# Placing the read-back of softmax sums, the loads of their reciprocals, and h's block sums in a hybrid decoder block

## The chip, the cores and the metric

The kernel runs on one core of a Trainium2 chip. The metric is the device time of one execution in microseconds; lower is better. The profile of one execution gives the times of single instructions, in microseconds from the start of its span.

## The reference

One decoder block on a sequence of L = 16 + 1024 tokens (16 learned tokens ahead of 1024 real ones), width D = 1024, all in float32:

```python
h = rmsnorm(x, norm_g)
u_pool, z_pool, q, k, v, z_attn, f_logit, g_pool, g_attn = split(h @ w_in)
y_pool = causal_multiscale_pool(u_pool, pool_w, pool_scale) * silu(z_pool)     # windows 2, 4, 8, 16
log_f  = log_sigmoid(f_logit + b_forget)
y_attn = forgetting_attention(q, k, v, log_f) * silu(z_attn)                    # 8 heads of 64, causal softmax
merged = sigmoid(g_pool) * (y_pool @ w_up_pool) + sigmoid(g_attn) * (y_attn @ w_up_attn)
out    = rmsnorm(x + merged @ w_out, final_norm_g)[16:]
```

In the attention, logits are q.k/8 plus a running sum of log forget gates, and each row is divided by the sum of its exponentials. That division is what the first part of the change is about: the kernel forms the undivided outputs first and multiplies them by the reciprocals of the sums much later.

## The kernel before

**Precision.** Every float32 product is made of three matmuls: each operand is split into a rounded part (ScalarE copies it) and the rest (VectorE or GpSimd subtracts), and rounded×rounded, rounded×rest and rest×rounded are added up in PSUM.

**Start (lines 460 to 578).** Eight tiles of 128 tokens (and one of 16) are loaded (`norm_load`), normalised, transposed by TensorE and split into `hh` and `hl`. For each tile `norm_stat` lets ScalarE sum the squares and GpSimd form the root (`rstd`), then `norm_scale` (VectorE, two operations at L258) scales it, and `norm_t` transposes it (TensorE at L279), rounds it (ScalarE, `hh` at L281) and subtracts (VectorE, `hl` at L282). Between these stand the first head pair's projections: `todo` lists (q, k, v) for four stretches of tokens, twelve steps numbered n = 0 to 11. In this stretch each engine works its instructions in program order. Steps 4 to 11 also call `h_block`: VectorE adds or negates a block of `hh` and `hl` into a tile `f` (L174 or L176, 1024 columns wide) and SyncE stores it to DRAM (L177), for products formed later in a seven-product (Strassen-like) way. Step 4 besides issues the loads `wf`, `bfb`, `psc` and the next q weights (`early["q"]`), step 6 the next k weights, step 8 forms `wfs` from `wf`; each of steps 4 to 11 issues one DRAM to DRAM copy (`copies(1)`).

**Attention (lines 580 to 881).** Sixteen units (four head pairs, two heads, two halves of the queries). TensorE's idle time in a unit is filled with projections. The sums of exponentials of each unit go as `acc` to DRAM (`accd`).

**The seven rounds (lines 896 to 1251).** The remaining gates z and g are projected by seven rounds n of products over 512×512 blocks. `order` lists products (n, i), i = 0 to 5; 38 of the 42 stand in the loop below, the last four come after it. Each product is 12 matmuls of 128×512 (L1069). All engines work in program order here, SyncE's queue of transfers too:

```python
for x, e in enumerate(order[:38]):
    if x == 0:
        g_prod(order[0])
        g_prod(order[1])
    if 4 <= x + AH < 42:
        split_next(order[x + AH])     # AH = 4: weights of the product four further on
    if x + 2 < 38:
        g_prod(order[x + 2])          # TensorE: the product two further on
    for f in before.get(e, ()):
        f()
    run_due(x)
    if x:
        evict(order[x - 1])           # clears the bank of the product before
    if x % 3 == 2:
        g_flush()
    for f in extra.get(e, ()):        # what hangs on this chunk
        f()
```

`split_next` (w_split) rounds a product's weights on ScalarE (L1024) and subtracts on GpSimd (L1031) or, for every third product, on VectorE (L1028); when half a load is used up it issues the next load of weights (`graw`, L1012). `g_prod` writes to one of eight PSUM banks: products with i < 4 of rounds 0, 2, 5 and 6 have a bank of their own (`ga_`), all others go round four banks (`gb_`), so that product (3,2) uses the bank of (2,4), and (4,5) that of (4,1). `evict` clears a bank on ScalarE (L1074) for rounds 0, 3 and part of 2, and on VectorE (L1080) for (2,4), (2,5) and rounds 1, 4 and 5; round 4's are followed by a sum on GpSimd (L136). `h_in(n)` loads round n's blocks of h (L1017) and `h_split(n)` splits them (L1040, L1045).

The tables `before` and `extra` hang other work on the chunks. For the softmax sums these are:

```python
def sums_in():
    for p in range(4):
        nc.sync.dma_start(lall[32 * p:32 * p + 32], sums[4 * p:4 * p + 4]....)     # L990
def sums_out():
    nc.vector.tensor_reduce(rall..., lall..., axis=AX.X, op=ALU.add)                # L994
    nc.vector.reciprocal(rall, rall)                                                # L996
    nc.vector.transpose(fin[:, 320:], rall)                                         # L997
    nc.sync.dma_start(recs.rearrange("(b p) r -> p b r", p=128), rect)              # L998
def rc_in(p):
    RC[p] = rc = gp.tile([128, SEQ], F32, name="rc", tag="g")
    for e in range(2):
        rw = recs...[4 * e + p:4 * e + p + 1]
        nc.sync.dma_start(rc[rows(e)[0]], rw.to_broadcast([64, SEQ]))               # L929
def attn_norm(p):
    nc.vector.tensor_tensor(Y[p], Y[p], RC[p], op=ALU.mult)                         # L932
```

Ahead of them, `acc_in(k)` and `acc_sum(k)` for k = 0 to 7, from (0,1) to (2,0), read `accd` back, sum over the keys, and with k = 7 store `sums` to DRAM (L986); `sums_in` follows in (2,0). `attn_in(p)` loads the undivided outputs `Y[p]` (L917, L920), and `attn_out(p)`, which needs `attn_norm(p)`, comes after the rounds. `pool_chain(g)` (one step for each call of `steps_of`) and `pool_split(g)` form the pooling branch's operands on VectorE and ScalarE (L951, L958, L965, L966). Tiles `u`, `s2`, `y`, `rc`, `plh` and `pll` share a ring of 13 slots, tag "g".

**End (lines 1253 to 1480).** The up-projections with their gates, and the last product with the final norm.

Of the kernel before, what the change touches and what calls it, by code (L numbers as in the profile page):

```python
# [44 lines left out]
def r32(ap):  # L45
    return ap.bitcast(F32)
# [7 lines left out]
def tile_hybrid_block(ctx, tc, x, meta, norm_g, w_in, b_forget, pool_w, pool_scale,  # L54
# [98 lines left out]
    def hblock(d, blk):  # L153
        r, c = int(blk[0]) - 1, int(blk[1]) - 1
        return r32(d[c][:, :, 512 * r:512 * r + 512])

    def rows_of(t):
        return t.rearrange("(k p) c -> p k c", p=128)
# [11 lines left out]
    def h_block(blk, k):  # L170
        f = ap_.tile([128, 2, 512], F32, name="f", tag="s", bufs=6)
        hi, lo = [hblock(d, blk)[:, k:k + 2] for d in (hh4, hl4)]
        if blk in ("12", "21"):
            nc.vector.scalar_tensor_tensor(f, hi, -1.0, lo, op0=ALU.mult, op1=ALU.subtract)  # L174
        else:
            nc.vector.tensor_tensor(f, hi, lo, op=ALU.add)  # L176
        nc.sync.dma_start(rows_of(HS[{"12": "C", "21": "X"}.get(blk, blk)])[:, k:k + 2], f)  # L177
# [59 lines left out]
    def run(g):  # L237
        for _ in g:
            pass
# [4 lines left out]
    def norm_load(i):  # L244
        c0 = i * 128
        n = min(128, L - c0)
        xt = ap_.tile([128, D], F32, name="xt", tag="s", bufs=6)
        nc.sync.dma_start(xt[:n], meta if n < 128 else x2[c0:c0 + n, :])
        return xt
# [40 lines left out]
    def zero_q(p):  # L290
        for e in range(2):
            nc.gpsimd.memset(r32(QL[p, e])[rows(e)[1]], 0.0)
# [18 lines left out]
    def q_piece(p, w, c0, c1):  # L311
        ps = yield from g_proj(w, c0, c1)

        def hi(e, r):
            nc.scalar.activation(QA[p, e][r, c0:c1], ps[rows(e)[0]], AF.Copy, scale=0.125)

        def lo(e):
            a, _ = rows(e)
            nc.vector.scalar_tensor_tensor(QL[p, e][a, c0:c1], ps[a], 0.125, r32(QA[p, e][a, c0:c1]),
                                           op0=ALU.mult, op1=ALU.subtract)  # L320

        for e in range(2):
            hi(e, rows(e)[0])
            hi(e, rows(e)[1])
        for e in range(2):
            lo(e)

    def k_piece(p, w, t0, t1):
        ps = yield from g_proj(w, t0, t1)
        for e in range(2):  # L330
            a, o = rows(e)
            for c, d in keys_of(t0, t1):
                nc.scalar.activation(KA[p, e][a, d], ps[a, c], AF.Copy)
        for e in range(2):
            a, o = rows(e)
            for c, d in keys_of(t0, t1):
                nc.vector.tensor_tensor(KA[p, e][o, d], ps[a, c], r32(KA[p, e][a, d]), op=ALU.subtract)  # L337

    def v_piece(p, w, t0, t1):
        ps = yield from g_proj(w, t0, t1)  # L340
        for c, d in keys_of(t0, t1):
            nc.scalar.activation(VT[p][:, d], ps[:, c], AF.Copy)

    def v_alloc(p):
        for e in range(2):
            V[p, e] = ap_.tile([KB, NB, 2, 64], F32R, name="V", bufs=3)
# [138 lines left out]
    def split_hi(raw, pool, tag):  # L485
        hi = pool.tile([128, KO, 128], F32R, name="whi", tag=tag)
        nc.scalar.activation(hi, raw, AF.Copy)
        return hi
# [13 lines left out]
    def ntok(i):  # L502
        return min(128, L - 128 * i)
# [22 lines left out]
    for n, (kind, t0, t1) in enumerate(todo):  # L526
        if n + 4 < 8:
            xts[n + 4] = norm_load(n + 4)
        if kind == "q":
            run(q_piece(0, wq, t0, t1))  # L530
        elif kind == "k":
            run(k_piece(0, wk, t0, t1))
        else:
            g = v_piece(0, wv, t0, t1)
            run(g)
        i = {0: 2, 1: 3, 3: 4, 4: 5, 5: 8, 6: 6, 7: 7}.get(n)
        if i is not None:
            norm_t(i, xts[i], ntok(i))
        if n == 0:
            hv_ = split_hi(rv, gp, "g")  # L540
            wv = split_lo(rv, hv_, gp, "g")
            VT[0] = gp.tile([128, L], F32, name="vt", tag="g")
            v_alloc(0)
        i = {1: 4, 2: 5, 3: 8, 4: 6, 5: 7}.get(n)
        if i is not None:
            norm_scale(xts[i], ntok(i), norm_stat(xts[i], ntok(i)))
        if n == 2:
            zero_q(0)
        if n == 4:
            wf = at_.tile([128, KO, H], F32, name="wf", bufs=1)  # L550
            nc.sync.dma_start(wf, w_in2[:, :, COL_F:COL_F + H])
            nc.sync.dma_start(bfb, bass.AP(tensor=b_forget.tensor, offset=b_forget.offset, ap=[[0, 128], [1, H]]))
            nc.sync.dma_start(psc, pool_scale[0].rearrange("(g c) -> c g", c=128))
        if n == 8:
            wfs = at_.tile([128, KO, 2 * H], F32R, name="wfs", bufs=1)
            nc.vector.tensor_copy(wfs[:, :, :H], wf)
            nc.vector.tensor_tensor(wfs[:, :, H:], wf, r32(wfs[:, :, :H]), op=ALU.subtract)
        if n == 4:
            early["q"] = load_raw(COL_Q + 128)
        if n == 6:  # L560
            early["k"] = load_raw(COL_K + 128)
        if n > 3:
            h_block(("11", "12", "22", "21")[n // 2 - 2], n % 2 * 2)
            copies(1)
        if n == 7:
            pw = ap_.tile([128, 4, 128], F32, name="pw", tag="s", bufs=6)
            nc.sync.dma_start(pw, pool_w[0].rearrange("g c d -> c g d"))
        if n == 10:
            nc.scalar.activation(pwh, pw, AF.Copy)
            nc.gpsimd.tensor_tensor(pwl, pw, r32(pwh), op=ALU.subtract)  # L570
        if n in (4, 7, 10):
            run(v_blocks(0, *range(max(1, 2 * (n // 3) - 2), 2 * (n // 3))))
# [341 lines left out]
    def attn_in(p):  # L914
        y = gp.tile([128, SEQ], F32, name="y", tag="g")
        if p == 3:
            nc.sync.dma_start(y, spill["y", p])  # L917
        else:
            for e in range(2):
                nc.sync.dma_start(y[rows(e)[0]], spill["y", p][:64, SEQ * e:SEQ * e + SEQ])  # L920
        Y[p] = y
# [3 lines left out]
# [3 lines that stand above are left out]
            rw = recs.rearrange("(h c) r -> h (c r)", h=H)[4 * e + p:4 * e + p + 1]  # L928
# [4 lines that stand above are left out]
# [29 lines left out]
    def pool_split(g):  # L962
        u = chains[g][0]
        plh, pll = [gp.tile([128, SEQ], F32R, name=n, tag="g") for n in ("plh", "pll")]
        nc.scalar.activation(plh, u[:, NM:], AF.Copy)  # L965
        nc.vector.tensor_tensor(pll, u[:, NM:], r32(plh), op=ALU.subtract)  # L966
        chains[g] += [plh, pll]
# [46 lines left out]
    def h_in(n):  # L1014
        raw_h[n] = [wp.tile([128, 2, 512], F32, name="hraw", tag=t) for t in ("wh", "wl")]
        for k in range(2):
            nc.sync.dma_start(raw_h[n][k], rows_of(HSRC[n])[:, 2 * k:2 * k + 2])  # L1017
# [18 lines left out]
    def h_split(n):  # L1036
        op_h[n] = [[hq.tile([128, 2, 512], F32R, name="gh", tag="h") for _ in range(2)] for _ in range(2)]
        hi, lo = op_h[n]
        for k in range(2):
            nc.scalar.activation(hi[k], raw_h[n][k], AF.Copy, scale=-1.0 if n == 2 else 1.0)  # L1040
        for k in range(2):
            if n == 2:
                nc.vector.scalar_tensor_tensor(lo[k], raw_h[n][k], -1.0, r32(hi[k]), op0=ALU.mult, op1=ALU.subtract)
            else:
                nc.vector.tensor_tensor(lo[k], raw_h[n][k], r32(hi[k]), op=ALU.subtract)  # L1045
# [144 lines left out]
    def steps_of(g):  # L1190
        return lambda: next(g, None)

    c2_, c1_ = pool_chain(2), pool_chain(1)
# [15 lines left out]
        (2, 1): [steps_of(c2_), lambda: attn_in(2)],  # L1209
        (2, 2): [steps_of(c2_), steps_of(c1_)],  # L1210
        (2, 3): [steps_of(c1_), lambda: h_in(5)],
        (2, 4): [steps_of(c1_), sums_out, lambda: attn_in(3)],
        (2, 5): [lambda: rc_in(0), lambda: rc_in(1)],
        (3, 0): [steps_of(c0_)],
        (3, 1): [lambda: h_split(4)],
        (3, 2): [steps_of(c0_)],
        (3, 3): [lambda: pool_split(3)],
        (3, 4): [lambda: attn_norm(0), lambda: h_in(6)],
        (3, 5): [lambda: pool_split(2)],
        (4, 0): [lambda: attn_norm(1)],  # L1220
        (4, 1): [lambda: h_split(5)],
        (4, 2): [lambda: rc_in(2)],
        (4, 3): [lambda: pool_split(1)],
        (4, 4): [lambda: rc_in(3)],
        (5, 3): [lambda: h_split(6)],
# [283 lines left out]
```

## Time and profile before

| | |
|---|---|
| median of 3 runs | 729.25 us (725.02, 729.25, 729.87) |
| profiled execution, own time | 727.64 us |
| its span | 725.9 us |
| mean granted TensorE clock | 0.994 |
| TensorE busy | 708.0 us (98%) |
| VectorE, ScalarE, GpSimd busy | 518.1, 421.0, 343.4 us |
| seven rounds' products | about 410 to 556 us |

The span runs from the first instruction of the program to the last; the own time holds 1.7 us besides. In the timelines a row gives start, duration, engine, line, operation, what is written and read, shapes and count, and in brackets how long the engine was idle before and what ended that. PE is TensorE, PEld its weight loads, DVE is VectorE, ACT is ScalarE, POOL is GpSimd, SPq is SyncE's queue of transfers. A row can merge several instructions; its duration is then that of all.

### The profile page before, as it was taken

The page shows a single profiled execution, that of the slowest core. Times are in us where ns is not written, and L with a number is a line of the kernel's source. Part 1 is how long each engine was busy: PE and PEld are TensorE (multiplying, and loading weights), DVE is VectorE, ACT ScalarE, POOL GpSimd, SP SyncE. Part 2 cuts the span into 40 slices and gives each one's busy share as a digit, 9 for nine tenths or more (in the row PEclk, how much of TensorE's full clock was granted, in tenths as well). Part 3 has the DMA queues.
Part 4 walks back from the last instruction along what each step waited for, and adds up shares of the span by engine and source line. Part 5 has one row for each costly group of instructions (what it writes and reads, how often), then busy time and mean ns, then how long its engine had stood idle before and what let it go on. Part 6 is the DMA issues. An engine that isn't in the chain of part 4 may idle for free.

```text
span 725.9 us, 10889 instructions
## 1 busy us (share of the span) xinstructions
PE 708.0 (98%) x3613; PEld 610.9 (84%) x3613; DVE 518.1 (71%) x917; ACT 421.0 (58%) x928; POOL 343.4 (47%) x463
## 2 busy tenths in 40 slices
PE   8989999999999999999999999969999999999996
PEld 6987999998899888998888888848888888888885
DVE  5774488576888868786876927957857645888775
ACT  7654477676767768676667522445545423525445
POOL 5423247476275847466395922346982010006152
PEclk9999999999999999999999999989999999999999
DMA  9299977956534475546648369689607367771006
GB/s 310 45 273 357 330 258 175 214 121 161 127 100 101 134 207 118 145 102 158 167 133 223 84 228 315 181 223 329 183 30 258 113 223 247 247 246 59 0 1 232
DMA packets 95354, 129.89 MB, mean 179 GB/s; under 512 B 11457, under 2 KB 62657, under 8 KB 93266
## 3 DMA queue, kind: packets, MB, share of 16 engines
q1 hardware_dynamic: 91776, 110.32, 48.1%
q0 software_dynamic: 2224, 16.25, 12.0%
q10 hardware_dynamic: 1298, 2.63, 1.0%
q8 instruction: 28, 0.46, 0.3%
q14 instruction: 28, 0.23, 0.1%
HBM read 102.25 MB, written 58.39 MB: 221 GB/s over the span
## 4 chain that ended last, share of the span: by engine, by line
PE 85%; DMA 5%; DVE 5%; ACT 2%; issue 2%; POOL 0%; SPq 0%; POOLq 0%; ACTq 0%; DVEq 0%
PE pj L217 53%; PE pj L1389 8%; PE pj L1069 7%; PE po L793 5%; PE pt L1389 2%; PE pt L1069 2%; PE ps L729 2%; PE ps L728 2%; DMA sums<-ge 1%; DMA zp<-accd 1%; DMA graw<-gs 1%; PE pj L589 1%; PE pt L279 1%; DVE pl L775 1%; PE pj L729 1%
## 5 line engine op out<-in xcount | busy, mean ns | idle before, releaser
L217 PE MATMUL pj<-hh,whi 128*128 128x512 f32 (+3 forms) x576 | 127.2, 347 | 0.3 <-DVE ka L337 0.2
L217 PE MATMUL pj<-hh,wlo 128*128 128x512 f32 (+3 forms) x576 | 127.2, 346 | 0.0
L217 PE MATMUL pj<-hl,whi 128*128 128x512 f32 (+3 forms) x576 | 126.8, 345 | 0.0
L217 PEld LDWEIGHTS pj<-hh,whi 128*128 128x128 f32 x576 | 97.3, 188 | 10.8 <-PE pj L217 0.5
L217 PEld LDWEIGHTS pj<-hh,wlo 128*128 128x128 f32 x576 | 96.8, 188 | 10.0
L217 PEld LDWEIGHTS pj<-hl,whi 128*128 128x128 f32 x576 | 96.5, 188 | 9.7
L208 POOL TENSOR_TENSOR wlo<-raw,whi 128x256 fp32r<-128x256 f32 x100 | 74.4, 775 | 63.9 <-PE pj L217 22.3
L783 POOL TENSOR_TENSOR acc<-acc,S 128x256 f32<-128x256 f32 (+2 forms) x128 | 90.6, 727 | 8.3 <-ACT S L770 4.1
L775 DVE TENSOR_TENSOR pl<-S,ph 128x512 fp32r<-128x512 f32 (+4 forms) x112 | 79.9, 735 | 15.6 <-ACT ph L774 14.9
L1031 POOL TENSOR_TENSOR gw<-graw,gw 128x256 fp32r<-128x256 f32 x52 | 49.1, 970 | 56.0 <-ACT gw L1024 55.9
L1069 PE MATMUL pj<-gh,gw 128*128 128x512 f32 x276 | 66.4, 398 | 7.2 <-DVE gx L1080 7.2
L1069 PEld LDWEIGHTS pj<-gh,gw 128*128 128x128 f32 x276 | 53.2, 193 | 18.8 <-issue 7.5
L742 DVE TENSOR_TENSOR pt<-pt,S 128x400 f32<-128x400 f32 (+2 forms) x96 | 46.6, 485 | 20.0 <-ACT S L733 17.7
L770 ACT ACTIVATE S<-S 128x512 f32<-128x512 f32 (+4 forms) x112 | 50.2, 481 | 12.2 <-DVE S L769 12.0
L774 ACT ACTIVATE ph<-S 128x512 fp32r<-128x512 f32 (+4 forms) x112 | 52.6, 482 | 3.1 <-PE po L793 2.2
L769 DVE TENSOR_TENSOR S<-S,pt 128x512 f32<-128x512 f32 (+4 forms) x112 | 49.9, 497 | 0.6
L1024 ACT ACTIVATE gw<-graw 128x512 fp32r<-128x512 f32 x38 | 23.3, 624 | 38.7 <-DMA graw<-gs 19.1
L1282 DVE TENSOR_TENSOR rl<-pj,rl 128x512 f32<-128x512 f32 x32 | 22.0, 689 | 28.6 <-PE pj L217 28.0
L783 POOL TENSOR_TENSOR acc<-S 128x256 f32<-128x256 f32 (+1 forms) x32 | 29.5, 949 | 23.6 <-ACT S L770 20.5
L733 ACT ACTIVATE S<-ps,negc 128x16 f32<-128x16 f32 (+4 forms) x65 | 33.1, 514 | 10.8 <-PE ps L729 10.3
L793 PE MATMUL po<-ph,V 128*128 128x512 f32 (+4 forms) x112 | 36.4, 325 | 0.0
L1389 PE MATMUL pj<-opw 128*128 128x512 f32 (+1 forms) x168 | 36.2, 374 | 0.0
(249 smaller groups left out, 1393.7 us busy)
## 6 DMA issues: line engine op xcount, KB each, us to landing
raw<-in_w_in_dram SPq DMA_DIRECT2D x27, 512.0 KB, 6.7
gs<-in_w_in_dram SPq DMA_DIRECT2D x15, 512.0 KB, 9.7
gs<-gs POOLq DMA_DIRECT2D x4, 1536.0 KB, 13.0
graw<-gs SPq DMA_DIRECT2D x12, 512.0 KB, 7.0
td<-in_w_out_dram SPq DMA_DIRECT2D x10, 512.0 KB, 11.3
graw<-in_w_in_dram SPq DMA_DIRECT2D x9, 512.0 KB, 5.9
xt<-in_x_dram SPq DMA_DIRECT2D x8, 512.0 KB, 7.0
accd<-acc SPq DMA_DIRECT2D x16, 256.0 KB, 2.6
```

Of the source, the lines that this page charges most:

```text
L208: ins = nc.gpsimd.tensor_tensor(lo[:, k:k + 2], raw[:, k:k + 2], r32(hi[:, k:k + 2]), op=ALU.subtract)
L217: nc.tensor.matmul(ps, a, b, start=(i == 0), stop=(i == len(seq) - 1))
L742: nc.vector.tensor_tensor(m[:kb, c0:], m[:kb, c0:], s[:kb, c0:], op=ALU.max)
L769: nc.vector.tensor_tensor(s[:kb, c0:], s[:kb, c0:], self.pm[:kb, c0:], op=ALU.subtract)
L770: exps.append(nc.scalar.activation(s[:kb, c0:], s[:kb, c0:], AF.Exp))
L774: nc.scalar.activation(ph[:kb, c0:], s[:kb, c0:], AF.Copy)
L775: dves.append(nc.vector.tensor_tensor(pl[:kb, c0:], s[:kb, c0:], r32(ph[:kb, c0:]), op=ALU.subtract))
L783: accs.append(nc.gpsimd.tensor_tensor(acc[:kb, c:c1], (S0 if b == 1 else acc)[:kb, c:c1], s[:kb, c:c1], op=ALU.add))
L793: nc.tensor.matmul(self.po[:, c0:], v, self.P[b][i][:kb, c0:], start=(b == 0 and i == 0), stop=(b == self.nb - 1 and i == 1))
L1031: nc.gpsimd.tensor_tensor(op[:, 1, k:k + 2], raw[:, k:k + 2], r32(op[:, 0, k:k + 2]), op=ALU.subtract)
L1069: nc.tensor.matmul(ps, stat(n, i, p, k), op_h[n][q][k // 2][:, k % 2], start=fresh and m == 0, stop=m == 11, skip_group_check=True)
L1389: nc.tensor.matmul(ps, pick(A_, k, p)[:, i * 128:(i + 1) * 128], pick(B_, k, q)[:, c0:c1], start=start and n == 0, stop=n == 11, skip_grou ...
```

## The change

In the start, `h_block` of steps 4 to 11 is called ahead of the step's `norm_scale`, and so ahead of the loads, of `wfs` and of the copy that the step issues, instead of after them. In the seven rounds, `sums_out` goes from (2,4) to (3,1), behind `h_split(4)`; `rc_in(0)` and `rc_in(1)` from (2,5) to (3,3), behind `pool_split(3)`; `attn_norm(0)` from (3,4) to (4,1), ahead of `h_split(5)`; and `attn_norm(1)` from (4,0) to (4,2), ahead of `rc_in(2)`. No operation is added or removed.

```diff
@@ -541,6 +541,8 @@
             VT[0] = gp.tile([128, L], F32, name="vt", tag="g")
             v_alloc(0)
+        if n > 3:
+            h_block(("11", "12", "22", "21")[n // 2 - 2], n % 2 * 2)
         i = {1: 4, 2: 5, 3: 8, 4: 6, 5: 7}.get(n)
         if i is not None:
             norm_scale(xts[i], ntok(i), norm_stat(xts[i], ntok(i)))
@@ -560,7 +562,6 @@
             early["k"] = load_raw(COL_K + 128)
         if n > 3:
-            h_block(("11", "12", "22", "21")[n // 2 - 2], n % 2 * 2)
             copies(1)
@@ -1209,17 +1210,16 @@
         (2, 3): [steps_of(c1_), lambda: h_in(5)],
-        (2, 4): [steps_of(c1_), sums_out, lambda: attn_in(3)],
-        (2, 5): [lambda: rc_in(0), lambda: rc_in(1)],
+        (2, 4): [steps_of(c1_), lambda: attn_in(3)],
         (3, 0): [steps_of(c0_)],
-        (3, 1): [lambda: h_split(4)],
+        (3, 1): [lambda: h_split(4), sums_out],
         (3, 2): [steps_of(c0_)],
-        (3, 3): [lambda: pool_split(3)],
-        (3, 4): [lambda: attn_norm(0), lambda: h_in(6)],
+        (3, 3): [lambda: pool_split(3), lambda: rc_in(0), lambda: rc_in(1)],
+        (3, 4): [lambda: h_in(6)],
         (3, 5): [lambda: pool_split(2)],
-        (4, 0): [lambda: attn_norm(1)],
-        (4, 1): [lambda: h_split(5)],
-        (4, 2): [lambda: rc_in(2)],
+        
+        (4, 1): [lambda: attn_norm(0), lambda: h_split(5)],
+        (4, 2): [lambda: attn_norm(1), lambda: rc_in(2)],
         (4, 3): [lambda: pool_split(1)],
```

## The prediction

> **What bounds the kernel now.** I read the page first: TensorE is busy for 98% of the span, so what counts is the time in which it stands still or runs slowly. A measurement of this kernel tells about 1% (7.3 us of the 729.25 us median) from no change.
>
> ```profile
> PE 708.0 (98%) x3613; PEld 610.9 (84%) x3613; DVE 518.1 (71%) x917; ACT 421.0 (58%) x928; POOL 343.4 (47%) x463
> ```
>
> The view of waits, for TensorE alone and from 43 us on, and the clock by stretches say where it stands still:
>
> ```profile
> PE pj L1069 <- DVE gx L1080: 7.2, 1, 7.2
> PE pt L279 <- DVE hl L282: 1.8, 1, 1.8
> PE pj L217 <- DVE ka L337: 0.2, 1, 0.2
> ...
> 41.00:44.00 3.00, 1.22 (x11) 1.19 (x11) 2.95 (x6) 1.48 (x4) 0.00 (x0) 1.00 0.66 197
> 488.00:492.00 4.00, 3.99 (x10) 3.17 (x11) 4.00 (x4) 1.64 (x3) 1.82 (x2) 0.50 1.04 345
> 488.01:498.42 10.41, 10.41 (x37) 8.48 (x38) 7.82 (x7) 4.82 (x8) 4.83 (x4) 0.80 1.06 341
> 498.42:509.30 10.88, 10.88 (x50) 9.01 (x49) 8.76 (x7) 7.17 (x10) 8.62 (x6) 1.00 1.06 317
> ```
>
> Columns of a stretch: from:to, length, busy time of PE, PEld, DVE, ACT, POOL, then granted clock, DMA share, GB/s. TensorE loses 7.15 us once (at 488) and 1.78 us once (at 42). After the long stop its clock is 0.50 until about 492: the three products of 488.01 to 498.42 take 10.41 us, where four at full clock take 10.88 (2.72 each, 8.16 for three). So the long stop costs 7.15 + 2.25 = 9.4 us. After the short one the clock is 1.00.
>
> The timelines around 488 name the cause (start, length, engine, line, operation, count, idle time before and releaser):
>
> ```profile
> 471.09 1.62 SPq L986 DMA_DIRECT2D sums<-ge  x1
> 481.19 1.93 SPq L990 DMA_DIRECT2D fin<-sums  x4
> 476.73 1.23 DVE L958 SCALAR_TENSOR_TENSOR u<-s,u 128x1024 f32<-128x1024 f32 x1
> 485.25 0.58 DVE L994 TENSOR_REDUCE fin<-fin 128x64 f32<-128x256 f32 x1 [7.29 <-DMA fin<-sums]
> ...
> 486.62 0.65 DVE L1028 TENSOR_TENSOR gw<-graw,gw 128x512 fp32r<-128x512 f32 x1
> 487.19 1.28 DVE L1080 TENSOR_TENSOR gx<-pj,gx 128x512 f32<-128x512 f32 x2
> 479.39 1.69 ACT L1024 ACTIVATE gw<-graw 128x512 fp32r<-128x512 f32 x3
> 488.01 10.41 PE L1069 MATMUL pj<-gh,gw 128*128 128x512 f32 x36 [7.15 <-DVE gx L1080]
> ```
>
> The sums of exponentials go to DRAM at 471.09 and land 10.1 us later; the read back lands at about 485.2. VectorE is idle from 477.96 because `sums_out` (L994) stands at the head of its queue. Behind it stand the split of product (3,3)'s weights (486.62; product (n,i) is the i-th of six in round n) and the eviction of (2,4) (487.19). Product (3,2) reuses (2,4)'s bank, so TensorE waits from 480.86 to 488.01.
>
> **The change part by part.** Part one moves `sums_out` from (2,4) to the end of (3,1). VectorE, free at 477.96, next meets (3,3)'s split, which needs ScalarE's rounding (first of the three at 479.39, done at 480.0): 480.06 + 0.57 to the next start, the first eviction 480.63 to 481.3, and TensorE starts 0.14 later (before: the first eviction, 0.68 long, ended at 487.87). New wait 481.45 − 480.86 = 0.6 us: **saved 6.55**. With a stop that short I take no half clock: **saved 2.25** more. The three small operations of `sums_out` (485.25 to 486.6) lie now behind (4,0)'s split of h; by then their data has landed (485.2), so they cost VectorE 1.4 us with nothing behind them before 488.
>
> The Trainium skill, "TensorE: Matmul & The Clock Gate", section "Part 1: The HAM clock gate", says that one idle window of about 3.4 us puts the clock to half until about 3.4 us of work have passed; the 7.15 and 1.78 us stops above agree. By it a new stop that crosses such a window would bring the half clock back; that is the first rival below.
>
> What is late next is **VectorE behind the reciprocals**. The same edits send `rc_in(0)` and `rc_in(1)` from (2,5) to (3,3), and `attn_norm(0)` from (3,4) to (4,1), where it stands ahead of `h_split(5)`, of the split for (5,3) and of the eviction of (4,1), for which product (4,5) waits (banks go round by four).
>
> ```profile
> 486.46 1.03 SPq L1017 DMA_DIRECT2D hraw<-hsX  x2
> 487.59 0.56 SPq L998 DMA_DIRECT2D recs<-fin  x1
> 488.40 0.34 SPq L917 DMA_DIRECT2D y<-sp_y  x1
> 489.19 0.37 SPq L1012 DMA_DIRECT2D graw<-in_w_in_dram  x1
> 494.87 2.81 SPq L929 DMA_DIRECT2D rc<-recs  x4
> 497.72 1.14 SPq L1012 DMA_DIRECT2D graw<-gs  x2
> DMA to landing us min/median/max: 7.2/7.2/7.2
> DMA to landing us min/median/max: 6.8/7.3/7.8
> DMA to landing us min/median/max: 7.6/7.6/7.6
> DMA to landing us min/median/max: 4.5/4.8/5.1
> DMA to landing us min/median/max: 3.8/5.3/9.7
> 484.00:504.00 20.00, 15.99 (x62) 13.12 (x63) 13.97 (x15) 9.70 (x15) 8.23 (x7) 0.83 1.03 299
> ```
>
> The five landing lines (time from issue, for each line's transfers) are those of the store to `recs`; of the two loads of h before it; of the load of y at 488.40; of rc's first two loads; and of all eight of rc. From 484 to 504 the DMA engines are full (1.03), and landings come in order of issue: h at 493.3 and 494.65, recs at 494.8, y at 496.0, about 1.35 us for each 512 KB. SyncE's queue: recs now comes after y, the load at 489.19, and one more 512 KB load of weights (issued at 497.72 before, since it stood behind rc's wait; now at about 489.2). Estimate from those landings: y 495.9, two loads at 1.35 each to 498.6, recs 498.8 instead of 494.8. rc's first two loads go out at 498.9 and 499.4; the median 4.8 us, with little queued ahead (one load), gives 503 to 504, bounds 502.7 by the fastest, 3.8, and 509 by the slowest, 9.7. I take 503.5, where `attn_norm(0)` starts; in the old trace it is 500.54.
>
> ```profile
> 500.54 1.23 DVE L932 TENSOR_TENSOR y<-y,rc 128x1024 f32<-128x1024 f32 x1 [4.71 <-DMA rc<-recs]
> 501.68 1.23 DVE L1028 TENSOR_TENSOR gw<-graw,gw 128x512 fp32r<-128x512 f32 x1
> 506.79 2.89 DVE L1045 TENSOR_TENSOR gh<-hraw,gh 128x1024 fp32r<-128x1024 f32 x2
> 511.51 2.42 POOL L136 TENSOR_TENSOR zp<-zp 128x256 f32<-128x256 f32 x2 [1.23 <-DVE zp L1080]
> 522.85 7.82 POOL L1031 TENSOR_TENSOR gw<-graw,gw 128x256 fp32r<-128x256 f32 x6
> ```
>
> After it on VectorE: 1.14 for itself (500.54 to 501.68), 2.3 for h's two splits (1.14 each beside an idle GpSimd; 2.89 beside a busy one), 0.6 for a split, 0.7 for the eviction (487.19, two in 1.28): done at 508.2, TensorE on at 508.35. TensorE, without its stop, has run nine products from 481.45: 481.45 + 9 × 2.72 + 0.1 (the bank of (3,5) is cleared behind a weight load landing at 488.4) = 506.0. **New wait 2.4 us.** Then GpSimd's chain (511.51 on), released by that eviction, starts 3.2 us earlier, while products run 6.3 us earlier. Its splits for (5,4) and (5,5), six pieces from 522.85, were done by about 525.3 and 528.2, and their products began at 528.3 and 531.1 (seven and eight products after 509.30): 3 us to spare become none, **0.4 us**, bounds 0 and 2. rc(2), rc(3) and the loads behind them keep their places. The slots of the shared "g" ring stay enough: before `pool_split(2)` at most 13 are held.
>
> Part two, the start. `h_block` moves ahead of `norm_scale` for n = 4 and 5; the later four moves change no order on VectorE but for two short casts.
>
> ```profile
> 38.73 1.41 DVE L258 SCALAR_TENSOR_TENSOR xt<-xt,rstd,gb 128x512 f32<-128x512 f32 x2 [1.78 <-POOL rstd L126]
> 40.05 1.22 DVE L176 TENSOR_TENSOR f<-hh,hl 128x1024 f32<-128x1024 f32 x1
> 41.19 0.85 DVE L319 SCALAR_TENSOR_TENSOR ql<-pj,qa 64x256 fp32r<-64x256 f32 x2
> 42.07 1.29 DVE L282 TENSOR_TENSOR hl<-pt,hh 128x512 fp32r<-128x512 f32 x2
> 42.81 0.66 PE L279 MATMUL pt<-ident,xt 128*128 128x128 f32 x4 [1.78 <-DVE hl L282]
> 17.90 0.44 SPq L482 DMA_DIRECT2D raw<-in_w_in_dram  x1
> 48.49 1.15 ACT L206 ACTIVATE whi<-raw 128x512 fp32r<-128x512 f32 x2 [1.53 <-PE pj L217]
> ```
>
> At n = 5 the 1.22 us block fills the 1.78 us in which VectorE waits for GpSimd, so what stood behind it (1.14 to the next start) comes 1.14 earlier, and with it the `hl` for which TensorE waits: **saved 1.1**, 0.6 of the stop remains. At n = 4 the two only change places and fill the same stretch; a delay there would add to TensorE's wait and is at most the block's 1.2 us. On SyncE the store of h passes four loads: they go out at about 35 to 37 instead of 16 to 18. The weights among them land after the median 6.7 us of that kind, near 44, and are first read at 48.49. From 43 to 488 TensorE has no stop above 0.22 us, so the 1.1 us is kept.
>
> **Sum:** −6.55 − 2.25 − 1.1 + 2.4 + 0.4 = **−7.1 us**. On the profiled execution's own 727.64 us that is 720.5; on the median, 722.1; the mean of the four times known (725.02, 727.64, 729.25, 729.87) is 728.0, which gives 720.9. I say 721.0.
>
> **Rivals.** (A) *The new wait grows past the clock's patience.* If rc lands 2 us later than I take, TensorE stops 4.4 us and pays the half clock again, 2.2 as after the old stop: 720.5 + 2.0 + 2.2 = 724.7. For it: full DMA engines; against it: rc's median. Chance 0.24. (B) *No new wait*: loads behind recs overtake nothing and rc lands as in the old trace, by 500.5 to 501: VectorE is ready before 506. Then 720.5 − 2.8 = 717.7. Chance 0.17. (C) *Slower*: the long wait only moves to (4,5). The savings are 9.9 us; with 0.4 and 2.2 for the clock, it decides from a stop of 7.3 us, that is rc landing after 508.4. With the slowest landing of 9.7 us it comes at 509.1: a stop of 8.0, time 728.3. Chance 0.05. (D) *The start gains nothing*, because `hl` at 42.07 is held by ScalarE's `hh` and not by its queue (the chain names ScalarE there): 721.6, within the forecast's range; it changes no chance.
>
> **How the numbers follow.** Forecast 0.52 (719 to 723), A 0.24, B 0.17, C 0.05, 0.02 for something else. 717 to 726 holds the forecast, B and A. Faster by over 1% (below 722.0): two thirds of the forecast and all of B, 0.53; slower by over 1%: 0.03, the far end of C; the rest 0.44.
>
> **What would show it.** TensorE's wait for `gx` L1080 at 0.6 us or less, no half clock near 490; VectorE idle before `y` L932 for about 6 us; a TensorE wait of 2 to 3 us on `zp` L1080 in n = 4; the wait on `hl` L282 at 0.6. It is wrong if recs lands before the two weight loads ahead of it, if a stop of over 4 us is left, or if a load gives a new wait between 43 and 480.

## The result and the profile after

Six executions of each kernel on one chip gave 727.82 us before (725.02 to 729.87) and 722.03 us after (719.3 to 722.76): a ratio of 0.9916, interval 0.9887 to 0.9945. That is 5.8 us less on the medians; 721.0 us (717 to 726) was forecast. The profiled execution of the changed kernel took 722.76 us, 4.9 us less than the profiled one before (727.64).

The page of the changed kernel, and its view of TensorE's waits (what waited and for what: us in total, times, longest):

```profile
span 721.0 us, 10896 instructions
PE 707.9 (98%) x3613; PEld 610.3 (85%) x3613; DVE 517.5 (72%) x917; ACT 419.8 (58%) x928; POOL 340.6 (47%) x463
PE pj L1070 <- ACT zp L1078: 3.4, 1, 3.4
PE pn L472 <- DVE car L626: 1.3, 1, 1.3
PE pt L279 <- DVE hl L282: 0.8, 1, 0.8
```

The lines of the rounds are one higher than before (L1069 is now L1070, L1080 is L1081, L932 is L933, and so on). The work is the same; the wait of 7.2 us for `gx` is gone, the one for `hl` is 0.8 instead of 1.8, and a wait of 3.4 us stands where there was none. That new wait is at product (4,5). The view names ScalarE's write of `zp` as what ended it; the timelines below put an eviction by VectorE just ahead of it too, and an experiment (e3) shows that this is what TensorE waited for.

TensorE's stretches around both places (columns as in the prediction: from:to, length, busy PE, PEld, DVE, ACT, POOL, granted clock, DMA share, GB/s):

```profile
477.20:480.00 2.80, 2.80 (x14) 2.19 (x13) 1.86 (x3) 2.80 (x6) 2.66 (x4) 1.00 0.11 10
504.65:508.03 3.38, 0.00 (x2) 0.03 (x1) 3.38 (x5) 3.35 (x5) 0.07 (x1) 1.00 1.02 366
508.03:508.94 0.91, 0.91 (x4) 0.78 (x5) 0.91 (x2) 0.45 (x1) 0.91 (x1) 1.00 1.09 353
508.94:512.35 3.41, 3.41 (x10) 2.62 (x9) 3.41 (x6) 0.98 (x2) 3.41 (x3) 0.50 1.09 265
512.35:516.00 3.65, 3.65 (x17) 3.01 (x17) 3.21 (x4) 1.06 (x3) 3.65 (x5) 1.00 1.09 244
```

Where the old stop began, TensorE now has no idle time. It stands still from 504.65 to 508.03, and 0.91 us after it has started again the clock goes to 0.50 for 3.41 us.

The changed kernel's timelines of VectorE, ScalarE and TensorE at those places:

```profile
476.47 0.63 ACT L1025 ACTIVATE gw<-graw 128x512 fp32r<-128x512 f32 x1 [5.71 <-DMA graw<-gs]
478.14 1.02 DVE L1029 TENSOR_TENSOR gw<-graw,gw 128x512 fp32r<-128x512 f32 x1 [2.37 <-ACT gw L1025]
479.08 1.28 DVE L1081 TENSOR_TENSOR gx<-pj,gx 128x512 f32<-128x512 f32 x2
479.93 8.40 PE L1070 MATMUL pj<-gh,gw 128*128 128x512 f32 x36
...
503.18 1.23 DVE L933 TENSOR_TENSOR y<-y,rc 128x1024 f32<-128x1024 f32 x1 [6.89 <-DMA rc<-recs]
504.32 2.35 DVE L1046 TENSOR_TENSOR gh<-hraw,gh 128x1024 fp32r<-128x1024 f32 x2
506.60 0.68 DVE L1029 TENSOR_TENSOR gw<-graw,gw 128x512 fp32r<-128x512 f32 x1
507.20 0.69 DVE L1081 TENSOR_TENSOR zp<-pj,zp 128x512 f32<-128x512 f32 x1
508.03 4.57 PE L1070 MATMUL pj<-gh,gw 128*128 128x512 f32 x12 [3.38 <-ACT zp L1078]
512.44 2.90 PE L1070 MATMUL pt<-gh,gw 128*128 128x512 f32 x12
```

VectorE waits 6.89 us for `rc`, then works through `attn_norm(0)`, the two splits of h, the split for (5,3) and the eviction of (4,1). TensorE starts 0.14 us after that eviction ends (507.89). The product that then starts takes 4.57 us, the one after it 2.90: that difference, 1.7 us, is the price of the half clock.

SyncE's queue of transfers shows why `rc` comes at 503 (the last two lines are the times from issue to landing of `recs` and of rc's first two loads):

```profile
486.13 0.51 SPq L918 DMA_DIRECT2D y<-sp_y  x1
486.69 1.30 SPq L1013 DMA_DIRECT2D graw<-in_w_in_dram  x1
488.03 0.54 SPq L1013 DMA_DIRECT2D graw<-gs  x1
489.63 1.97 SPq L999 DMA_DIRECT2D recs<-fin  x1
498.45 2.37 SPq L930 DMA_DIRECT2D rc<-recs  x4
DMA to landing us min/median/max: 8.8/8.8/8.8
DMA to landing us min/median/max: 3.5/3.8/4.1
```

The 32 KB store to `recs` now stands behind the load of y and two loads of weights, and lands 8.8 us after its issue, at 498.44; rc's loads go out at once.

Comparing the starts of TensorE's 3613 instructions one with another gives the account. After the stop for `hl` the changed kernel is 1.09 us ahead; 0.31 of that is lost up to 145 us, most of it at 143.7, where a weight load of the attention waits 0.28 us for VectorE (L738); the old stop and its half clock bring 9.28 more; the new stop costs 3.51 with the small gaps beside it, its half clock 1.69. So −0.78 − 9.28 + 3.51 + 1.69 = −4.86, and it stays so to the end (−4.9).

### The profile page after: what moved, and what is told of

Read it like the earlier page. It is cut to its first block, busy times and chain, and to the rows that moved or that the text cites. A ratio compares the mean times of both kernels' runs of the same rounds, so it can differ in the third digit from the quotient of the medians.

```text
span 721.0 us, 10896 instructions
## 1 busy us (share of the span) xinstructions
PE 707.9 (98%) x3613; PEld 610.3 (85%) x3613; DVE 517.5 (72%) x917; ACT 419.8 (58%) x928; POOL 340.6 (47%) x463
## 4 chain that ended last, share of the span: by engine, by line
PE 93%; DVE 3%; ACT 2%; issue 1%; POOL 0%; POOLq 0%; ACTq 0%; DVEq 0%
PE pj L217 53%; PE pj L1070 12%; PE pj L1389 8%; PE po L794 5%; PE pt L1070 4%; PE pt L1389 2%; PE ps L730 2%; PE ps L729 2%; PE pj L590 1%; DVE pl L776 1%; PE pt L279 1%; PE pj L730 1%; PE pj L729 1%; ACT qa L315 1%; PE pn L279 0%
## 5 line engine op out<-in xcount | busy, mean ns | idle before, releaser
L1032 POOL TENSOR_TENSOR gw<-graw,gw 128x256 fp32r<-128x256 f32 x52 | 46.7, 928 | 52.8 <-ACT gw L1025 52.6
L1070 PE MATMUL pj<-gh,gw 128*128 128x512 f32 x276 | 66.2, 397 | 3.4 <-ACT zp L1078 3.4
L1070 PEld LDWEIGHTS pj<-gh,gw 128*128 128x128 f32 x276 | 52.6, 191 | 15.1 <-ACT zp L1078 3.8
```

Of the source, the lines that this page charges most:

```text
L1032: nc.gpsimd.tensor_tensor(op[:, 1, k:k + 2], raw[:, k:k + 2], r32(op[:, 0, k:k + 2]), op=ALU.subtract)
L1070: nc.tensor.matmul(ps, stat(n, i, p, k), op_h[n][q][k // 2][:, k % 2], start=fresh and m == 0, stop=m == 11, skip_group_check=True)
```

## The experiments

The theory: the time went down because VectorE no longer waits for `fin` ahead of the eviction of (2,4), and what came back is VectorE's wait for rc ahead of the eviction of (4,1). Rivals: the view is right in naming ScalarE at (4,5); the start brings most of the gain; it is the loads' new order in the queue, not VectorE's, that counts. Each kernel was timed beside the kernel before on the same chip, in three sets: e1, e3, e5 and e6; e2, e3 again, e4 and the changed kernel again (e7); e8, e10, e3 and the changed kernel a third time. The kernel before took 726.01, 727.07 and 726.45 us (medians) in these sets.

### The start alone (e1)

The kernel before, with only `h_block` moved:

```diff
+        if n > 3:
+            h_block(("11", "12", "22", "21")[n // 2 - 2], n % 2 * 2)
         i = {1: 4, 2: 5, 3: 8, 4: 6, 5: 7}.get(n)
...
         if n > 3:
-            h_block(("11", "12", "22", "21")[n // 2 - 2], n % 2 * 2)
             copies(1)
```

> The kernel before with the first part alone (h_block ahead of norm_scale). My theory: TensorE's wait on hl L282 at 42 us falls from 1.78 to about 0.77 us as in the changed kernel, and 0.8 to 1.1 us of it reach the end; the stop at 488 stays near 7 us with its half clock. Time 0.5 to 1.5 us below the kernel before. Rival (hl is held by ScalarE or the start is hidden later): no change, ratio 1.000, wait on hl still 1.8.

Measured: 725.96 us (724.81 to 726.66), ratio 0.9998, interval 0.9984 to 1.0012. No gain can be told, though the wait on `hl` fell as in the changed kernel; the interval reaches down to 0.9984, which is 1.2 us, so it does not exclude the gain that I expected either. TensorE's waits and two stretches of this kernel:

```profile
PE pj L1070 <- DVE gx L1081: 4.5, 1, 4.5
PE pt L279 <- DVE hl L282: 0.8, 1, 0.8
481.25:485.74 4.49, 0.00 (x1) 0.03 (x1) 2.69 (x6) 0.46 (x2) 0.26 (x1) 0.93 0.92 206
485.74:491.91 6.17, 6.17 (x15) 4.82 (x16) 6.17 (x6) 2.09 (x5) 2.40 (x2) 0.50 1.05 360
```

The long stop, behind `sums_out`, is still there with its half clock: TensorE stands still and then runs 6.17 us at 0.50. The stop ends when a transfer lands, not a fixed time after TensorE gets there: here the store of the sums went out at 468.82 instead of 471.09 and the stop ended at 485.74 instead of 488.01, both 2.27 us sooner, although TensorE came to it 0.4 us later. In this profiled execution the first loads landed 1.1 us later than in the profile before, which the 1.0 us at `hl` made good. My explanation, that the stop took the gained time back, is not shown by this: in these two profiles the landing itself moved by more than the gain. By itself the move at the start is worth nothing that these 12 executions can tell.

### The rounds alone (e2), beside the changed kernel again (e7)

The changed kernel with `h_block` back in its old place (the reverse of the diff above), and the changed kernel itself.

> The changed kernel without the first part (h_block behind norm_scale as before). My theory: the first part alone gave nothing because the long stop, which ends with the landing of the sums, took the 1.0 us back; behind the changed rounds nothing takes it back in full, but the stop at (4,5), which ends with the landing of rc, takes part of it. So this is 0 to 1 us slower than the changed kernel. Rival 1 (the start's gain is lost before the rounds): no difference. Rival 2 (gains add up): 1.0 us or more slower.

> The changed kernel again, beside the three kernels of this call on the same chip. Theory and rivals alike: 5 to 6 us below the kernel before, a stop of 2 to 4 us at (4,5), in some executions with a half clock behind it.

Measured: e2 722.96 us (719.79 to 725.3), ratio 0.994, interval 0.9918 to 0.9962; the changed kernel 721.76 us (720.15 to 722.62), ratio 0.993, interval 0.9913 to 0.9946. So the rounds bring most of it (4.1 of 5.3 us on the medians); the 1.2 us between the two lies within the intervals, and can't tell my theory (0 to 1 us) from the rival that the gains add up (1.0 us or more). The wait and two stretches of e2, which has no line shift of one:

```profile
PE pj L1069 <- ACT zp L1077: 3.6, 1, 3.6
506.06:509.67 3.61, 0.00 (x1) 0.03 (x1) 3.61 (x5) 3.56 (x5) 0.07 (x1) 1.00 1.04 350
509.67:513.00 3.33, 3.33 (x15) 2.76 (x16) 3.33 (x5) 0.45 (x1) 3.33 (x3) 1.00 1.13 302
```

A stop of 3.61 us here is followed by full clock, where 3.38 us in the profile above were followed by half: see the last section. The changed kernel's profile of this set has the same wait at 2.4 us, also without half clock.

### The sums' read-back alone put back (e5)

```diff
-        (2, 4): [steps_of(c1_), lambda: attn_in(3)],
+        (2, 4): [steps_of(c1_), sums_out, lambda: attn_in(3)],
...
-        (3, 1): [lambda: h_split(4), sums_out],
+        (3, 1): [lambda: h_split(4)],
```

> The changed kernel with sums_out alone put back to (2,4). My theory: VectorE again stands before the read back, TensorE stops 6 to 8 us on gx L1081 near 487 and runs at half clock after it; the wait at (4,5) goes or shrinks, since TensorE comes later and rc sooner. Time about that of the kernel before less the start's 0.8: 726 to 728. Rival (the gain comes from the loads of rc being out of the way of the weights): the time stays near 722.

Measured: 725.84 us (722.62 to 728.59), ratio 0.9999, interval 0.998 to 1.0017. Without this one step of the change the whole gain is gone. TensorE's longest wait in this kernel:

```profile
PE pj L1070 <- DVE gx L1081: 6.0, 1, 6.0
```

The old stop is back, 6.04 us of it, with half clock behind it, and there is no wait at (4,5): TensorE comes there late enough.

### VectorE's order at (4,1) (e3, in each of the three sets)

The changed kernel with `attn_norm(0)` behind `h_split(5)` and behind the eviction for which (4,5) waits. No other engine's order and no transfer's place changes:

```diff
-        (4, 1): [lambda: attn_norm(0), lambda: h_split(5)],
-        (4, 2): [lambda: attn_norm(1), lambda: rc_in(2)],
+        (4, 1): [lambda: h_split(5)],
+        (4, 2): [lambda: attn_norm(0), lambda: attn_norm(1), lambda: rc_in(2)],
```

> The changed kernel with attn_norm(0) taken from (4,1) to (4,2), ahead of attn_norm(1), so that it stands behind h_split(5) and the eviction of (4,1). My theory: the 3.38 us stop of product (4,5) in the changed kernel comes from that eviction, queued on VectorE behind attn_norm(0), which waits for rc; so the stop goes, its half clock (1.7 us) with it, and the time falls by 4 to 5 us to about 717.5. Rival (the releaser the view names, ScalarE's zp L1078, is the true one): the stop stays at about 3.4 us and the time at 722.

> attn_norm(0) behind the eviction of (4,1), as in the run before, now beside the changed kernel. My theory: no stop above 0.5 us from 43 us to the end, no half clock in the rounds, 2.5 to 4.5 us below the changed kernel. Rival (TensorE's time after the rounds is bound by something else): within 1 us of the changed kernel.

> attn_norm(0) behind the eviction of (4,1) again, for comparison on the same chip with e8 and the changed kernel. Theory: 1.5 to 3 us below the changed kernel. Rival: equal to it.

Measured: 719.67, 719.98 and 719.49 us, ratios 0.9914 (0.989 to 0.9938), 0.9905 (0.9888 to 0.9921) and 0.9905 (0.9889 to 0.9922). The changed kernel, on the same chip in the second and third set, took 721.76 and 721.66 us (ratio of the third 0.9945, interval 0.9924 to 0.9965). So this version beats both kernels: its 15 executions of all sets have their median at 719.52, the changed kernel's 11 of two sets at 721.76, 2.2 us or 0.3% apart. From the third one's view of waits and the timelines of VectorE, TensorE and ScalarE:

```profile
PE pj L217 <- DVE zp L906: 0.8, 1, 0.8
502.78 0.68 DVE L1081 TENSOR_TENSOR zp<-pj,zp 128x512 f32<-128x512 f32 x1
503.38 1.21 DVE L933 TENSOR_TENSOR y<-y,rc 128x1024 f32<-128x1024 f32 x1
502.09 5.60 PE L1070 MATMUL pj<-gh,gw 128*128 128x512 f32 x24
507.52 0.63 ACT L1078 ACTIVATE zp<-zp 128x512 f32<-128x512 f32 x1
```

The eviction of (4,1) now comes ahead of `attn_norm(0)` and does not wait for rc. The products (4,4) and (4,5) run back to back, 24 matmuls in 5.60 us, so that (4,5) starts at about 504.8. ScalarE's write of `zp` (L1078), which the view had named, comes only at 507.52, when (4,5) is nearly done; so TensorE does not wait for it, it was VectorE's eviction that held (4,5), and the theory stands. I expected more time from it than came (4 to 5 us, then 2.5 to 4.5). Two things were left out: the stop in the changed kernel is not always 3.4 us (2.42 and 2.65 in its profiles of the second and third set), and in two of the three sets some of the gain is taken back in the pooling product, where TensorE now waits for `zp` (0.8 us here, 0.3 in the first set, nothing of note in the second).

### The reciprocals' products in their old places (e4)

The changed kernel with `attn_norm(0)` back in (3,4) and `attn_norm(1)` in (4,0), so that VectorE meets rc's wait earlier:

```diff
-        (3, 4): [lambda: h_in(6)],
+        (3, 4): [lambda: attn_norm(0), lambda: h_in(6)],
...
-        (4, 1): [lambda: attn_norm(0), lambda: h_split(5)],
-        (4, 2): [lambda: attn_norm(1), lambda: rc_in(2)],
+        (4, 0): [lambda: attn_norm(1)],
+        (4, 1): [lambda: h_split(5)],
+        (4, 2): [lambda: rc_in(2)],
```

> The changed kernel with attn_norm(0) and attn_norm(1) back at (3,4) and (4,0), while sums_out and the loads of rc stay further on. My theory: attn_norm(0) now stands ahead of the split for (4,3) on VectorE, and waits for rc until about 503; product (4,3), due at 499, waits until about 505, a stop of 5 to 6.5 us with a half clock of 2.2 us behind it: 2 to 4 us slower than the changed kernel, about the time of the kernel before. Rival (the place of attn_norm does not matter, only sums_out's): the same time as the changed kernel.

Measured: 726.27 us (723.62 to 727.6), ratio 0.9993, interval 0.998 to 1.0007. The whole gain is gone, 4.5 us against the changed kernel beside it where I expected 2 to 4, though not in one stop of 5 us or more:

```profile
PE pt L1070 <- DVE gw L1029: 3.5, 1, 3.5
PE pj L1070 <- DVE zp L1081: 0.8, 1, 0.8
503.84 1.23 DVE L933 TENSOR_TENSOR y<-y,rc 128x1024 f32<-128x1024 f32 x1 [11.89 <-DMA rc<-recs]
504.98 0.68 DVE L1029 TENSOR_TENSOR gw<-graw,gw 128x512 fp32r<-128x512 f32 x1
502.22:505.72 3.50, 0.00 (x0) 0.00 (x1) 1.88 (x3) 0.00 (x0) 0.00 (x0) 0.96 0.94 227
505.72:512.29 6.57, 5.77 (x13) 4.09 (x14) 6.57 (x6) 3.18 (x4) 3.32 (x2) 0.50 1.08 336
```

VectorE now waits 11.89 us for rc, and the split that (4,3) needs stands behind it. TensorE stops for 3.50 us at (4,3) and 0.8 at (4,4), and runs at half clock through the whole second stretch. The transfers stand in the queue as in the changed kernel, so their new order alone brings nothing. The two moves of the change belong together: `sums_out` moved later makes rc land later, and without the later `attn_norm` the stop only moves to another product. My size of that stop was wrong in its beginning: (4,3) came at 500.24 and not at 499, and its first eight matmuls, which do not use the part of the weights that VectorE subtracts, ran until 502.22.

### Getting rc sooner (e6, e10)

In e6 `sums_out` stands one chunk earlier than in the change, in (3,0), with `recs` ahead of one more load of weights; in e10 the load of the last y stands behind `recs`:

```diff
-        (3, 0): [steps_of(c0_)],
-        (3, 1): [lambda: h_split(4), sums_out],
+        (3, 0): [steps_of(c0_), sums_out],
+        (3, 1): [lambda: h_split(4)],
```

```diff
-        (2, 4): [steps_of(c1_), lambda: attn_in(3)],
+        (2, 4): [steps_of(c1_)],
...
+        (4, 0): [lambda: attn_in(3)],
```

> The changed kernel with sums_out one chunk sooner, at the end of (3,0), so that the store of recs goes ahead of one 512 KB load of weights. My theory (transfers land in order): recs and rc land about 1.4 us sooner, the stop at (4,5) falls from 3.4 to about 2.0 us, no half clock follows it, and the time falls by about 3 us to 719. Rival 1 (landing of rc does not hang on the order of the queue): stop still 3.4, time 722. Rival 2 (VectorE, waiting 1.5 us for the read back ahead of h_split(4), makes TensorE wait at (4,0)): time 722 to 724.

> The changed kernel with attn_in(3), a 512 KB load that stands ahead of recs and rc in the queue, taken from (2,4) to (4,0), behind them. My theory: rc lands when the bytes ahead of it have passed; 512 KB less, at 1.35 us each, bring it about 1.3 us sooner (seen from the landing of the sums), and the stop at (4,5) falls by as much, to 1 to 2 us, without a half clock: 1 to 2 us below the changed kernel beside it. Rival (rc's landing hangs on its own wait for recs and 3.5 us of latency, not on the bytes): no difference.

Measured: e6 721.48 us (718.14 to 723.9), ratio 0.9935, interval 0.9909 to 0.9961; e10 721.38 us (719.4 to 722.34), ratio 0.9932, interval 0.9914 to 0.995. Neither can be told from the changed kernel. SyncE's queue in e6, the landing times of rc's first two loads there, and the wait at (4,5) in e6 and in e10:

```profile
488.72 0.45 SPq L999 DMA_DIRECT2D recs<-fin  x1
489.21 3.22 SPq L1013 DMA_DIRECT2D graw<-gs  x2
496.91 2.37 SPq L930 DMA_DIRECT2D rc<-recs  x4
DMA to landing us min/median/max: 4.8/5.1/5.4
```

```profile
PE pj L1070 <- ACT zp L1078: 2.6, 1, 2.6
```

```profile
PE pj L1070 <- ACT zp L1078: 1.4, 1, 1.4
```

In e6 `recs` passes one load of weights and rc goes out 1.5 us sooner (496.91 against 498.45), but now two loads instead of one stand between `recs` and rc, whose first two loads take 4.8 to 5.4 us instead of 3.5 to 4.1. Counted from the landing of the sums, `attn_norm(0)` starts after 23.24 us in e6 and after 23.4 to 23.9 in three profiles of the changed kernel: I had expected 1.4 us, and some 0.4 came. In e10 the y load leaves the way altogether, that stretch is 22.36 us, and the wait at (4,5) is 1.4 us; but it shows as 0.3 us in the time, where I expected 1 to 2, and a wait of 0.3 us for `zp` is new in the pooling product.

### The best version without the start (e8)

The changed kernel with e3's two lines, and `h_block` in its old place.

> attn_norm(0) behind the eviction, as in e3, but h_block back behind norm_scale. My theory: the start's 1.0 us is real, and gave nothing alone because a stop that ends with a landing took it back; with no stop left in the rounds it shows in full, so this is 0.7 to 1.2 us slower than e3 beside it. Rival (the start's gain is lost before the rounds): equal to e3.

> The changed kernel again, for comparison on the same chip. Theory and rivals alike: 5 to 6 us below the kernel before.

Measured: 720.13 us (719.54 to 721.5), ratio 0.9921, interval 0.9904 to 0.9939; e3 beside it 719.49 (718.46 to 719.54), the changed kernel 721.66 (720.46 to 723.92). With no long stop left, the start's move shows as 0.6 us on the medians, where I expected 0.7 to 1.2 (0.78 us were left of the gain at the rounds in the account above): none of e3's five executions is above the lowest of e8's six, though the intervals of the ratios overlap. The waits of e8 for `hl` and `zp`:

```profile
PE pt L279 <- DVE hl L282: 1.8, 1, 1.8
PE pj L217 <- DVE zp L905: 0.5, 1, 0.5
```

## Why the prediction was right, step by step

**The base** was taken as 728.0 from four times; six executions gave 727.82. **The old stop.** Forecast: 6.55 of 7.15 us go, and 2.25 of clock. The runs: 9.28 in all, and no wait left at (3,2). The 0.6 us that I kept came from ScalarE's rounding, taken from the trace of before at 479.39. That rounding waited for a load of weights; in the profile after, ScalarE goes on from that load at 476.47 and VectorE starts its split at 478.14, 1.9 us sooner than I took. The split was longer, with GpSimd busy beside it (0.94 us to the next start, not 0.57; 0.65 us in all before, with GpSimd idle, and 1.02 now), and it still sufficed, with little to spare: one profile of e3 shows 0.4 us of that wait. e5 shows that this term hangs on the move of `sums_out`.

**The new wait at (4,5).** The place, the chain and its length were right: from the start of `attn_norm(0)` to the end of the eviction 4.71 us, where 4.7 was worked out. Forecast 2.4 us; three profiles of the changed kernel show 3.38, 2.42 and 2.65. `recs` was to land at 498.8 on the old clock, that is 497.7 with 1.1 us saved at the start; it landed at 498.44. rc was to be there at 503.5, or 502.4 with the same shift; VectorE starts at 503.18. Those 0.8 us, and TensorE arriving a little sooner (504.65 against 506.0 − 1.1 = 504.9), make the 3.38. The latency after the issue, which I bounded between 3.8 and 9.7, was 3.5 to 4.1, the fast end of the bounds: the second half of it, issued 0.5 us after the first, sets the end.

**The clock.** I took no half clock at this stop and gave it 0.24 as rival A, from a stop of 4.4 us. In one of three profiles it came with a stop of 3.38. The mean granted clock given with each execution tells more: of the changed kernel's 17 executions seven have 0.994 or 0.995, one 0.996, nine 0.997 to 0.999. In the three profiles the clock is also at half behind the last matmul, where it costs nothing, which takes 0.001 to 0.003 off the mean; a stretch of 3.41 us at (4,5) takes 0.0024. So the seven should be those with the half clock there; that is worked out from the means and was seen in one profile alone. Their median is 722.76, that of the nine 720.64. The step that was too simple is the one that let A start at 4.4 us. **This is the term that was mis-sized:** the sum of −7.1 has no clock in it, and in the execution compared, −4.9, there are 1.7 us of clock and 1.1 more of stop than forecast (3.51 with the small gaps); on the other side stand 0.5 us at the old stop and the 0.4 of GpSimd that wasn't seen (from 512 on the two kernels keep their distance of 4.9 us). At the start 0.3 was lost. −7.1 + 1.7 + 1.1 − 0.5 − 0.4 + 0.3 = −4.9. So it is partly luck that the median, 722.03, lies within 1.1 us of the 721.0 forecast: the half clock that the sum left out falls in some of the executions only, and two of the errors work against the other three.

The Trainium skill, "TensorE: Matmul & The Clock Gate", section "Part 1: The HAM clock gate", has the clock go to half after one idle window of about 3.4 us whose start is not tied to the kernel. It agrees with the runs in that the length alone doesn't decide (3.38 us halved the clock, 3.61 us in e2 didn't) and in the length of the half-clock stretch (3.41 us); it does not agree that the window must be idle throughout, as 2.5 us of it sufficed (last section).

**The start.** Forecast 1.1 saved; at `hl` 1.0 was saved (1.78 to 0.77), so rival D, that ScalarE's `hh` holds it, fell. "The 1.1 us is kept" does not hold in full: 0.31 us of it is lost up to 145 us, where the forecast had looked for stops above 0.22 us of TensorE's matmuls and a weight load now waits 0.28. Alone (e1) it is worth nothing that can be measured, in the changed kernel 1.2 us within the noise, in e8 against e3 0.6 us. Whether the long stop took the rest back in e1 is not shown; all three results agree with a worth of about 0.6 us.

**The other rivals.** B, that no new wait comes, fell: all three profiles have it, though e3 reaches by another order what B stood for. C, that the long stop only moves on, did not come with this change; e4 is nearly that case, and its time of 726.27 against 727.07 shows that the moves of `attn_norm` are what keeps it away. (A small slip: two thirds of 0.52 and 0.17 make 0.52, not the 0.53 given there for a fall of over 1%.)

## What to carry to other kernels

Where an engine works in program order, look for the instruction that waits for a long transfer and ask what stands behind it; move it behind the work for which the bounding engine waits, and then work out the same question at the place where it lands. A wait that the profile gives to one engine can be another's: an edit that takes away the wait of the one suspected, and the time at which the one named then finishes, settle it (e3). A gain early in the program has to be followed to the end: of the 1.09 us at the start, 0.78 were left when the rounds began.

## What the runs showed of the hardware

**Half clock comes in a grid.** In all these profiles the clock was at half for 3.41 us or twice that, never for another time up to the last matmul, and in each execution the trace's record of the granted clock changes on one grid of 3.41 us. In the profile after, the half stretch is 508.94 to 512.35, so the window before it is 505.53 to 508.94, and 2.50 us of it (505.53 to 508.03) were idle. In e2 a window's edge falls at 507.87, in the middle of the stop: 1.81 and 1.80 us of it lie in the two windows, and the clock stayed full. In e4 3.24 us of the 3.50 lay in one window, and it fell, as it did in e1, e5 and the kernel before, where a whole window was idle. The stops of 1.41, 2.42, 2.59 and 2.65 us had at most 1.79 in one window, and no half clock followed. The stretch behind the last matmul narrows it, as a window ends there at another place in each execution. From the changed kernel of the second set and from the kernel before:

```profile
711.65:713.77 2.12, 0.00 (x1) 0.00 (x0) 1.20 (x3) 1.24 (x4) 0.74 (x2) 1.00 0.44 160
713.77:717.00 3.23, 0.00 (x0) 0.00 (x0) 0.64 (x1) 0.60 (x1) 0.00 (x0) 0.50 0.85 311
719.14:720.90 1.76, 0.00 (x0) 0.00 (x0) 1.08 (x2) 1.12 (x3) 0.54 (x2) 1.00 0.45 164
720.90:724.31 3.41, 0.00 (x0) 0.00 (x0) 0.75 (x1) 0.72 (x1) 0.20 (x1) 1.00 0.84 308
```

With 2.12 us idle at its end a window was followed by half clock, with 1.76 it was not. So between 1.81 and 2.12 us of idle time in one window lies the point from which the clock fell in these runs; they don't say where. The way back took a window without idle time: in e1 a window whose first 0.66 us were idle was followed by a second at half, 6.83 us in all, as in the kernel before, e4 and e5, against 3.41 us in the changed kernel, whose first window at half was busy throughout. Where the grid lies against the stop differs from one execution to the next, and with it the time.

**A small store in a full queue takes as long as what is ahead of it.** The 32 KB of `recs` took 7.2 us before and 8.8 us after, rc's first two loads 3.5 to 4.1 us with one load of weights issued between `recs` and them, 4.8 to 5.4 with two (e6), and 9.3 to 10.1 in e5, with y and three loads of weights between. Passing loads with one transfer puts them in front of the next one, so a chain of two gains little (e6: 1.5 us for the first, some 0.4 for both); only a transfer taken off the way altogether brought rc sooner (e10).
